# Every second weight unit of two output projections: the low part from a negated copy and an adding DMA

## The chip, the core and the metric

The kernel runs on one core of one Trainium2 chip. The metric is device time in microseconds (us) of one execution; lower is better. The engines are TensorE (PE in the profile; its weight loads are PEld), VectorE (DVE), ScalarE (ACT), GpSimd (POOL) and SyncE (SP). Transfers that SP issues and transfers that POOL issues stand in the profile as queues q1 and q0; both run on the core's 16 DMA engines.

## The reference, cut to what matters

One decoder layer, 256 tokens by 2048 channels, float32. An input projection feeds two token mixers, latent attention and a short gated convolution. Each mixer's output (256 x 2048) goes through a 2048 x 2048 branch projection, the two are merged by sigmoid gates, and an output projection follows:

```python
y_mla  = einsum('bse,ed->bsd', attn, w_o_mla)
y_conv = einsum('bse,ed->bsd', b_gate * conv * silu(z_conv), w_o_conv)
merged = sigmoid(g_mla) * y_mla + sigmoid(g_conv) * y_conv
out    = einsum('bsd,de->bse', merged, w_out)
return x + rmsnorm(out, post_norm_g)
```

The change touches the weights of the first two products, `w_o_mla` and `w_o_conv`.

## The kernel before

**Products in two parts.** TensorE multiplies in float32r here. To keep the precision, every operand is split: `hi` is the value as it comes out when written to a float32r tile, `lo` is the rest (value minus `hi`), and a product is three matmuls, hi·hi, hi·lo and lo·hi (`product`, with the matmul at L90).

**Units of weights.** All weights come in units of at most 128 x 2048 float32 (1 MB), listed in `plan` in the order in which TensorE needs them. A unit goes through three steps: SP loads it into one of three `raw` buffers (`load_raw`, L161); ScalarE writes `whi` and VectorE writes `wlo` = raw - `whi` (`split_act`, L263 and L264), each into one of three slots of its own; TensorE uses the two. `take(i)` is called where unit i is used; it calls `ahead`, which first writes down the loads and splits of the units to come. Once written, each engine works through its own queue, and a step starts when its semaphores allow. A split may start when its slot is free, that is, when the last matmul of the unit three before is done; a load may start when the split of the unit three before is done.

**The stage of the change.** `tokens(c, n, cols)` runs the branch projections: n is the branch (0 latent attention, 1 convolution), c one of four blocks of 512 output channels, and four units (kk, 0 to 3) make up one block. That is 2 x 4 x 4 = 32 units, `u_d[n][c][kk]`, each used by 24 matmuls (two token halves, four blocks of 128 inputs, three matmuls each). I count these units from 0 to 31. The input `cols` is `x_both` (n = 0) or `cv_both` (n = 1). VectorE multiplies each finished block by its gate (L1005 and L1013, L1014). In branch 1 each merged block is also transposed: `turned` turns 32 x 32 pieces on VectorE (L338), sends them to DRAM in four transfers of 64 KB per token half (`far<-sg`, L345) and brings them back in one of 256 KB (`sg<-far`, L349), all issued by POOL and kept in the written order. `features` then splits them for the output projection (`x_both<-sg`).

**Order.** The matmuls, the turning transfers and some others stand in the order of the program; the rest is ordered by the framework's scheduler. Every engine runs its own queue in order.

Of the kernel before, what the change touches and what calls it, by code (L numbers as in the profile page):

```python
# [12 lines left out]
F32R = mybir.dt.float32r  # L13
I32 = mybir.dt.int32
AF = mybir.ActivationFunctionType
ALU = mybir.AluOpType
# [68 lines left out]
def tile_layer(ctx: ExitStack, tc: tile.TileContext, xw, x, pos, pvec, post_g, wc, wz, wcv, wkr, wqk, wqr, wv, cwr, wsq, wg, out):  # L85
    nc = tc.nc
# [21 lines left out]
    plan = []  # L108

    def add(ap, width=UNIT, kind="half"):  # L110
        plan.append((ap, width, kind))
        return len(plan) - 1
# [32 lines left out]
    u_d = [[[add(wsq[n, c, k], kind="whole") for k in range(4)] for c in range(4)] for n in range(2)]  # L145
# [2 lines left out]
    out_order += [(c, k) for c in (2, 3) for k in range(4)]  # L148
    u_out = {ck: add(wsq[2, ck[0], ck[1]], kind="whole") for ck in out_order}

    raws, splits, early = {}, {}, {}
    done = {"raw": 0, "split": 0}

    def load_raw(i):
        ap, w, _ = plan[i]
        t = early.get(i)
        if t is None:
            t = wpool.tile([P, UNIT], F32, name=f"raw{i}", tag="raw", bufs=3)
        cuts = {0: (S, XW, 2 * XW), 1: (0, XW, 2 * XW), 2: (0, XW, 2 * XW)}.get(i, (0, w))
        for a, b in zip(cuts[:-1], cuts[1:]):  # L160
            nc.sync.dma_start(out=t[:, a:b], in_=ap[:, a:b])  # L161
        raws[i] = t
        if i == u_ckv[1]:
            tc.keep_in_program_order(nc.sync.dma_start(out=x_tok, in_=x))

    def slot(i, both=True):
        hi = wpool.tile([P, UNIT], F32R, name=f"whi{i}", tag="whi", bufs=3)
        return hi, wpool.tile([P, UNIT], F32R, name=f"wlo{i}", tag="wlo", bufs=3) if both else None

    def split_unit(i):  # L170
        t, (_, w, kind) = raws.pop(i), plan[i]
        if i == u_kr:
            t = t[:, :w].rearrange("p (k c) -> p k c", k=KD)
            both, parts = slot(i, False)[0], []
            for h in range(2):
                part = both[:, h * HALF : (h + 1) * HALF].rearrange("p (k j c) -> p k j c", k=KD // 2, j=2)
                split_act(part[:, :, 0], part[:, :, 1], t[:, h * KD // 2 : (h + 1) * KD // 2])
                parts.append(part.rearrange("p k j c -> p k (j c)"))
            splits[i] = parts
            return  # L180
        if i <= u_qa[-1]:

            hi, lo = slot(i)
            for j in range(2):
                k, o = 2 * i + j, j * XW
                src = x_first if k == 0 else t[:, o : o + S]
                split_scaled(x_both, src, k)
                split_act(hi[:, j * R : (j + 1) * R], lo[:, j * R : (j + 1) * R], t[:, o + S : o + XW], True)
            splits[i] = hi, lo
            return  # L190
        if u_out[3, 0] <= i < u_out[3, 3]:
            hi, lo = (op.tile([P, UNIT], F32R, name=f"w{o}{i}") for o in ("hi", "lo"))
        else:
            hi, lo = slot(i)
        if kind == "pair":
            splits[i] = split_pair(i, t, hi, lo)
            return
        n = HALF if kind == "half" else UNIT
        for h in range(0, w, n):
            e = min(h + n, w)  # L200
            split_act(hi[:, h:e], lo[:, h:e], t[:, h:e])
        splits[i] = hi, lo

    def split_pair(i, t, hi, lo):

        raw = t[:, :].rearrange("p (b c) -> p b c", b=4)
        tf = d1.tile([P, 3, 512], F32, name=f"tf{i}", tag="tf", bufs=1)
        thi, tlo = (d1.tile([P, 3, 512], F32R, name=f"t{o}{i}", tag=f"t{o}", bufs=1) for o in ("hi", "lo"))
        tt = nc.vector.tensor_tensor
        tt(tf[:, :2], raw[:, 1:3], raw[:, 0:1].to_broadcast([P, 2, 512]), op=ALU.subtract)  # L210
        tt(raw[:, 0], raw[:, 2], tf[:, 0], op=ALU.add)
        tt(tf[:, 2], raw[:, 3], raw[:, 0], op=ALU.subtract)
        split_act(hi[:, :], lo[:, :], t[:, :])
        split_act(thi[:, :, :], tlo[:, :, :], tf[:, :, :])
        w = {}
        for n, b in ((6, 0), (1, 1), (3, 2), (2, 3)):
            w[n] = [a[:, b * 512 : (b + 1) * 512] for a in (hi, lo)]
        for n, b in ((5, 0), (7, 1), (4, 2)):
            w[n] = [a[:, b] for a in (thi, tlo)]
        return w  # L220

    def ahead(i, raw=3, split=1):
        while done["raw"] < min(i + raw, len(plan)):
            load_raw(done["raw"])
            done["raw"] += 1
        while done["split"] < min(i + 1 + split, len(plan)):
            while done["raw"] <= done["split"]:
                load_raw(done["raw"])
                done["raw"] += 1
            split_unit(done["split"])  # L230
            done["split"] += 1

    def take(i):
        ahead(i)
        parts = splits.pop(i)
        if isinstance(parts, dict):
            return parts

        def piece(j, n):
            return tuple(a[:, j * n : (j + 1) * n] for a in parts)  # L240

        return piece
# [19 lines left out]
    def split_act(hi, lo, src, keep=False):  # L262
        a = nc.scalar.activation(hi, src, AF.Copy)  # L263
        b = nc.vector.tensor_tensor(lo, src, hi.bitcast(F32), op=ALU.subtract)  # L264
        if keep:

            tc.keep_in_program_order(a)
            tc.keep_in_program_order(b)
# [53 lines left out]
    n = 2 * XW // S  # L322
# [37 lines left out]
    def split_scaled(dst, src, k):  # L360
        if k == 0:
            a = nc.vector.tensor_scalar(dst[:, k, :S], src, col("pre_g", k), None, op0=ALU.mult)
        else:
            a = nc.scalar.activation(dst[:, k, :S], src, AF.Copy, scale=col("pre_g", k))
        tc.keep_in_program_order(a)
        tc.keep_in_program_order(
            nc.vector.scalar_tensor_tensor(
                dst[:, k, S:], src, col("pre_g", k), dst[:, k, :S].bitcast(F32), op0=ALU.mult, op1=ALU.subtract
            )
        )  # L370
# [150 lines left out]
    for i in range(KD // 2):  # L521
        ahead(u_qa[i], raw=3 + len(early), split=0)
        w = take(u_qa[i])
        for j in range(2):
            latent_products(ps_q, 2 * i + j, w, j)
    ps_c = [bank(f"ckv{t}") for t in range(NT)]
    for i in range(4):
        w = take(u_ckv[i])
        for k4 in range(4):
            latent_products(ps_c, 4 * i + k4, w, k4)  # L530
        if i == 0:
            next(table_parts)
        if i == 1:
            dg = input_norm()
            latent_norm("qa", ps_q)
            next(table_parts)
# [34 lines left out]
    def group_a(g):  # L571

        qn, kn = pair("qn", (P, HG, S)), temp("kn", (P, 2, HG, S), F32R, 1)
        w = take(u_grp["a", g])
        for n, src, hi, lo in (("qn", qa, qn[0], qn[1]), ("kn", ckv, kn[:, 0], kn[:, 1])):
            for j, f in enumerate(narrow([f"{n}{g}_{j}" for j in range(HG)], w, HG * (n == "kn"), src)):
                split_act(hi[:, j, :], lo[:, j, :], f[:, :])
        groups["a", g] = qn, kn
# [629 lines left out]
```

## Time and profile before

| | |
|---|---|
| median of 3 runs | 1059.69 us (1058.46 to 1060.88) |
| the profiled execution | 1061.09 us, its span 1059.3 us |
| TensorE matmul busy | 1024.0 us, 97% |
| VectorE / ScalarE / POOL busy | 742.5 / 532.5 / 180.3 us |
| granted TensorE clock, mean | 0.988 |
| the stage of the change | about 790 to 964 us of the span |

The span is what the profiler saw between the first and the last instruction; 1.8 us of the profiled time lie around it. A row `L264 DVE TENSOR_TENSOR wlo<-raw,whi ... x32 | 73.3, 2289 | 71.9 <-ACT whi L263` reads: line 264, VectorE, `wlo` made from `raw` and `whi`, 32 times; 73.3 us busy, 2289 ns each; the engine was idle for 71.9 us in front of them, mostly until ScalarE's `whi` was there.

### The profile page before, as it was taken

The page shows a single profiled execution, that of the slowest core. Times are in us where ns is not written, and L with a number is a line of the kernel's source. Part 1 is how long each engine was busy: PE and PEld are TensorE (multiplying, and loading weights), DVE is VectorE, ACT ScalarE, POOL GpSimd, SP SyncE. Part 2 cuts the span into 40 slices and gives each one's busy share as a digit, 9 for nine tenths or more (in the row PEclk, how much of TensorE's full clock was granted, in tenths as well). Part 3 has the DMA queues.
Part 4 walks back from the last instruction along what each step waited for, and adds up shares of the span by engine and source line. Part 5 has one row for each costly group of instructions (what it writes and reads, how often), then busy time and mean ns, then how long its engine had stood idle before and what let it go on. Part 6 is the DMA issues. An engine that isn't in the chain of part 4 may idle for free.

```text
span 1059.3 us, 12469 instructions
## 1 busy us (share of the span) xinstructions
PE 1024.0 (97%) x4658; PEld 851.8 (80%) x4658; DVE 742.5 (70%) x960; ACT 532.5 (50%) x675; POOL 180.3 (17%) x345
## 2 busy tenths in 40 slices
PE   9999999999999999999999839999999999999997
PEld 8887888888878888788888728888888888888885
DVE  7578769686687777777677579797976445666462
ACT  7756546455465455455555145555565333334451
POOL 7621220204202042112422210000000000232000
PEclk9999999999999999999999969999999999999999
DMA  8754766667666685656767536655555555677842
GB/s 339 299 188 176 254 221 210 219 222 277 193 230 214 214 296 182 232 208 238 267 230 231 173 113 203 216 200 214 186 211 198 194 187 186 238 250 252 321 159 79
DMA packets 41948, 231.00 MB, mean 218 GB/s; under 512 B 7520, under 2 KB 8224, under 8 KB 18976
## 3 DMA queue, kind: packets, MB, share of 16 engines
q1 hardware_dynamic: 29808, 197.54, 52.4%
q0 software_dynamic: 11648, 29.38, 9.2%
q10 hardware_dynamic: 432, 3.29, 0.7%
q8 instruction: 36, 0.59, 0.2%
q14 instruction: 24, 0.20, 0.0%
HBM read 214.48 MB, written 11.53 MB: 213 GB/s over the span
## 4 chain that ended last, share of the span: by engine, by line
PE 90%; DVE 4%; issue 2%; DMA 2%; ACT 1%; POOL 1%; DVEq 0%; POOLq 0%
PE cv L90 28%; PE sq L90 16%; PE g L90 15%; PE z L90 8%; PE out L90 8%; PE qa L90 2%; PE qn L90 2%; PE ckv L90 2%; PE kn L90 2%; DMA cw<-cwr_dram 2%; PE vv L90 2%; PE sc L90 1%; DVE wlo L264 1%; ACT whi L263 1%; PE o L90 1%
## 5 line engine op out<-in xcount | busy, mean ns | idle before, releaser
L264 DVE TENSOR_TENSOR wlo<-raw,whi 128x1024 fp32r<-128x1024 f32 (+2 forms) x290 | 423.4, 1484 | 224.7 <-ACT whi L263 223.8
L263 ACT ACTIVATE whi<-raw 128x1024 fp32r<-128x1024 f32 (+2 forms) x292 | 357.5, 1259 | 380.3 <-issue 120.5
L90 PE MATMUL cv<-whi,x_both 128*128 128x512 f32 x1024 | 323.4, 390 | 3.3 <-DVE cv_w L726 3.3
L90 PEld LDWEIGHTS cv<-whi,x_both 128*128 128x128 f32 x1024 | 192.3, 188 | 43.5 <-DVE cv_w L726 4.3
L90 PE MATMUL cv<-wlo,x_both 128*128 128x512 f32 x512 | 199.7, 390 | 0.0
L90 PE MATMUL g<-whi,x_both 128*128 128x512 f32 x368 | 119.8, 390 | 0.0
L90 PEld LDWEIGHTS cv<-wlo,x_both 128*128 128x128 f32 x512 | 96.2, 188 | 18.7
L90 PEld LDWEIGHTS g<-whi,x_both 128*128 128x128 f32 x368 | 69.4, 189 | 14.4
L90 PE MATMUL z<-whi,x_both 128*128 128x512 f32 x256 | 80.6, 390 | 0.0
L90 PE MATMUL sq<-whi,x_both 128*128 128x512 f32 x256 | 79.0, 389 | 0.0
L90 PE MATMUL sq<-whi,cv_both 128*128 128x512 f32 x256 | 78.9, 389 | 0.0
L90 PE MATMUL out<-whi,x_both 128*128 128x512 f32 x256 | 78.9, 389 | 0.0
L345 POOL DMA_DIRECT2D far<-sg x32 | 17.5, 553 | 330.4 <-DVE sg L1014 287.8
L345 POOL DMA_DIRECT2D far<-via x64 | 35.3, 559 | 225.2 <-DVE via L338 224.2
L90 PE MATMUL g<-wlo,x_both 128*128 128x512 f32 x184 | 71.8, 390 | 0.0
L90 PEld LDWEIGHTS z<-whi,x_both 128*128 128x128 f32 x256 | 48.1, 188 | 9.9
L90 PEld LDWEIGHTS sq<-whi,cv_both 128*128 128x128 f32 x256 | 48.0, 188 | 9.9
L90 PEld LDWEIGHTS out<-whi,x_both 128*128 128x128 f32 x256 | 48.0, 188 | 9.9
L90 PEld LDWEIGHTS sq<-whi,x_both 128*128 128x128 f32 x256 | 48.0, 188 | 9.9
L90 PE MATMUL z<-wlo,x_both 128*128 128x512 f32 x128 | 49.8, 389 | 0.0
L90 PE MATMUL sq<-wlo,x_both 128*128 128x512 f32 x128 | 49.8, 389 | 0.0
L90 PE MATMUL sq<-wlo,cv_both 128*128 128x512 f32 x128 | 49.8, 389 | 0.0
(243 smaller groups left out, 1325.3 us busy)
## 6 DMA issues: line engine op xcount, KB each, us to landing
raw<-wcv_dram SPq DMA_DIRECT2D x64, 1024.0 KB, 5.1
raw<-wsq_dram SPq DMA_DIRECT2D x48, 1024.0 KB, 4.8
raw<-wg_dram SPq DMA_DIRECT2D x32, 1024.0 KB, 4.8
raw<-wz_dram SPq DMA_DIRECT2D x16, 1024.0 KB, 4.8
raw<-wqk_dram SPq DMA_DIRECT2D x8, 1024.0 KB, 5.6
cw<-cwr_dram POOLq DMA_DIRECT2D x24, 256.0 KB, 7.2
raw<-wc_dram SPq DMA_DIRECT2D x4, 1024.0 KB, 9.9
raw<-wv_dram SPq DMA_DIRECT2D x4, 1024.0 KB, 5.6
```

The lines of the kernel that those rows point to most:

```text
L90: return tc.keep_in_program_order(nc.tensor.matmul(*a, **kw))
L263: a = nc.scalar.activation(hi, src, AF.Copy)
L264: b = nc.vector.tensor_tensor(lo, src, hi.bitcast(F32), op=ALU.subtract)
L345: tc.keep_in_program_order(nc.gpsimd.dma_start(out=f[i], in_=m))
```

## The change

In the stage, the units with kk = 1 and 3 (the odd ones, 16 of 32) get their low part in another way. ScalarE makes `whi` as before, and writes -1 times the raw value into `wlo`; since `wlo` is float32r, this is -`whi`. Then POOL issues a DMA that reads the raw weights once more from DRAM and adds them onto `wlo`, which gives raw - `whi`. VectorE's subtraction for these units is gone. For the units from the stage's first up to the output projection's block 3, `ahead` also writes down loads four and splits two units ahead instead of three and one.

```diff
+    by_dma = {u_d[n][c][k] for n in range(2) for c in range(4) for k in (1, 3)}
...
+        if i in by_dma:
+            nc.scalar.activation(hi[:, :], t[:, :], AF.Copy)
+            nc.scalar.activation(lo[:, :], t[:, :], AF.Copy, scale=-1.0)
+            nc.gpsimd.dma_start(out=lo[:, :], in_=plan[i][0].bitcast(F32R), accum_op=ALU.add)
+            splits[i] = hi, lo
+            return
...
     def take(i):
-        ahead(i)
+        far_ahead = u_d[0][0][0] <= i < u_out[3, 0]
+        ahead(i, raw=3 + far_ahead, split=1 + far_ahead)
```

In the rows below, the number behind a name counts the program's tiles, and what a row waits for is named by the engine or DMA lane (DMASW for POOL's transfers, DMAHW for SP's) whose semaphore it needs. ScalarE before, in the middle of the stage, one row per unit:

```order
L263 ACTIVATE whi_6863<-raw_6831 128x2048 [waits DMAHW2_49,DVE_49,PE_49]
L263 ACTIVATE whi_6897<-raw_6861 128x2048 [waits DMAHW3_49,DVE_49,PE_49]
L263 ACTIVATE whi_6927<-raw_6895 128x2048 [waits DMAHW4_49,DVE_49,PE_49]
L263 ACTIVATE whi_6957<-raw_6925 128x2048 [waits DMAHW5_49,DVE_49,PE_49]
L263 ACTIVATE whi_6987<-raw_6955 128x2048 [waits DMAHW6_49,DVE_49,PE_49]
```

ScalarE now, at the same place (L271 is the old L263):

```order
L271 ACTIVATE whi_6845<-raw_6812 128x2048 [waits DMAHW2_49,PE_49,Activation_49]
L201 ACTIVATE wlo_6876<-raw_6843 128x2048 [waits DMASW7_49,DMAHW3_49,DVE_49,PE_49]
L200 ACTIVATE whi_6875<-raw_6843 128x2048 [waits PE_49,Activation_49]
L271 ACTIVATE whi_6910<-raw_6873 128x2048 [waits DMAHW4_49,PE_49,Activation_49]
L201 ACTIVATE wlo_6941<-raw_6908 128x2048 [waits DMASW0_49,DMAHW5_49,DVE_49,PE_49]
L200 ACTIVATE whi_6940<-raw_6908 128x2048 [waits PE_49,Activation_49]
```

Every second unit now has two rows, and the negative stands ahead of the rounded copy.

TensorE before, at the first unit of branch 1, where it takes up a new `whi` and a new `wlo`:

```order
L90 MATMUL sq_1_0_7017<-whi_6987,cv_both 128x512 [waits Activation_49]
L90 MATMUL sq_1_0_7017<-wlo_6988,cv_both 128x512 [waits DVE_49]
L90 MATMUL sq_1_0_7017<-whi_6987,cv_both 128x512 x2
L90 MATMUL sq_1_0_7017<-wlo_6988,cv_both 128x512
L90 MATMUL sq_1_0_7017<-whi_6987,cv_both 128x512 x2
```

TensorE now, at the second unit of branch 1 (an odd one):

```order
L90 MATMUL sq_1_0_7032<-whi_7001,cv_both 128x512 [waits Activation_49]
L90 MATMUL sq_1_0_7032<-wlo_7002,cv_both 128x512 [waits DMASW4_49]
L90 MATMUL sq_1_0_7032<-whi_7001,cv_both 128x512 x2
L90 MATMUL sq_1_0_7032<-wlo_7002,cv_both 128x512
L90 MATMUL sq_1_0_7032<-whi_7001,cv_both 128x512 x2
```

The second matmul of an odd unit no longer waits for VectorE but for a transfer that POOL issued. The order of the matmuls is the same in both programs.

POOL before, from the first merged block of branch 1 on; until then its queue has nothing in this stage:

```order
L345 DMA far<-sg 32x4x128 [waits DVE_49,Activation_49,Pool_49]
L345 DMA far<-sg 32x4x128 x3
L345 DMA far<-sg 32x4x128 [waits DVE_49]
L345 DMA far<-sg 32x4x128
L345 DMA far<-sg 32x4x128 [waits DMASW2_49]
L345 DMA far<-sg 32x4x128 [waits DMASW3_49]
L349 DMA sg<-far 128x512 [waits DMASW6_49,DMASW7_49,DMASW5_49,DMASW4_49]
L349 DMA sg<-far 128x512 [waits DMASW2_49,DMASW3_49,DMASW1_49,DMASW0_49]
```

POOL now, at the same place (L353 and L357 are the old L345 and L349, L202 is the adding DMA):

```order
L202 DMA wlo_7067<-wsq_dram 128x2048 [waits DMASW2_49,Activation_49]
L202 DMA wlo_7128<-wsq_dram 128x2048 [waits DMASW3_49,Activation_49]
L353 DMA far<-sg 32x4x128 [waits DVE_49,Pool_49]
L353 DMA far<-sg 32x4x128 x3
L353 DMA far<-sg 32x4x128 [waits DVE_49]
L353 DMA far<-sg 32x4x128 [waits DMASW4_49]
L353 DMA far<-sg 32x4x128 [waits DMASW5_49]
L353 DMA far<-sg 32x4x128 [waits DMASW6_49]
L357 DMA sg<-far 128x512 [waits DMASW2_49,DMASW7_49,DMASW1_49,DMASW0_49]
L202 DMA wlo_7209<-wsq_dram 128x2048 [waits Activation_49]
L357 DMA sg<-far 128x512 [waits DMASW5_49,DMASW6_49,DMASW4_49,DMASW3_49]
L202 DMA wlo_7270<-wsq_dram 128x2048 [waits Activation_49]
```

Eleven adding DMAs stand ahead of the first turning transfer, and the other five between the turning transfers; three of these (`wlo_7209` is the first) come behind one `sg<-far` and ahead of the next.

## The prediction, as put on record before the changed kernel ran

> **What bounds the kernel now.** I read the page's busy shares first, then the chain of work that ended last, then the stage of the change by groups, by engine and by queue.
>
> ```profile
> span 1059.3 us, 12469 instructions
> PE 1024.0 (97%) x4658; PEld 851.8 (80%) x4658; DVE 742.5 (70%) x960; ACT 532.5 (50%) x675; POOL 180.3 (17%) x345
> 628.14 162.30 PE g L90 x707
> 790.44 174.08 PE sq L90 x768
> 964.52 87.05 PE out L90 x384
> L264 DVE TENSOR_TENSOR wlo<-raw,whi 128x2048 fp32r<-128x2048 f32 x32 | 73.3, 2289 | 71.9 <-ACT whi L263 71.8
> L263 ACT ACTIVATE whi<-raw 128x2048 fp32r<-128x2048 f32 x32 | 61.3, 1917 | 100.1 <-PE sq L90 96.9 <-issue 3.0 <-ACT cv_both L263 0.2
> ```
>
> The first two rows are the page's: TensorE is busy 97% of the span. The next three are the end of the chain (start, length): from 628 us on it is TensorE alone, without a gap, and the branch projections (`sq`) are 174.08 us of it, 768 matmuls at 0.2267 us, 5.44 us per unit. The last two rows are groups of this stage alone: VectorE makes 32 low parts at 2.29 us and ScalarE 32 high parts at 1.92 us; ScalarE waits for TensorE to free slots. So VectorE, which the change relieves, is not what this stage waits for. A gain would need a TensorE wait that goes away, and there is none; what can change the time is a low part that comes late.
>
> How much room a low part has, from the timeline (start, length):
>
> ```profile
> 790.28 0.39 PE L90 MATMUL sq<-whi,x_both 128*128 128x512 f32 x1
> 790.50 0.39 PE L90 MATMUL sq<-wlo,x_both 128*128 128x512 f32 x1
> 834.00 1.92 ACT L263 ACTIVATE whi<-raw 128x2048 fp32r<-128x2048 f32 x1 [3.52 <-PE sq L90]
> 835.95 2.29 DVE L264 TENSOR_TENSOR wlo<-raw,whi 128x2048 fp32r<-128x2048 f32 x1 [1.26 <-ACT whi L263]
> ```
>
> Unit 0's first low matmul is at 790.50. Unit 7's last matmul ends at 790.28 + 191 x 0.2267 + 0.39 = 833.97, and ScalarE starts the split of unit 10, which takes unit 7's slot, at 834.00. Unit 10's first low matmul comes at 790.50 + 10 x 5.44 = 844.9. So a split has 10.9 us. Before, it used 4.24 of them (done at 838.24), with 6.7 us to spare.
>
> **The change part by part.**
>
> Removed: 16 subtractions of 2.29 us, 36.6 us of VectorE, all beside TensorE. Worth nothing on the path.
>
> Added on ScalarE: 16 negatives. The same engine, shape and number of operands as the row of 1.92 us, so 30.7 us, in a stage where ScalarE is idle for 100 us in front of its high parts alone. The high part of an odd unit now ends at 834.00 + 2 x 1.92 = 837.84 instead of 835.92; it is needed at 844.7. Nothing on the path.
>
> Loads: the raw buffer of an odd unit is freed by ScalarE at 837.84 instead of by VectorE at 838.24, 0.4 us earlier. SP's waits in the stage are only for these buffers, and a load lands in 4.8 us, some 7 us before unit 13's split at 850.3: covered. The longer look-ahead adds nothing of its own, since split and load already start when slots free them.
>
> Added on POOL: 16 adding DMAs of 1 MB. No row shows an adding DMA; these are the nearest, with the median time from issue to landing:
>
> ```profile
> raw<-wsq_dram SPq DMA_DIRECT2D x32, 1024.0 KB, 4.8
> far<-sg POOLq DMA_DIRECT2D x24, 64.0 KB, 3.0
> sg<-far POOLq DMA_DIRECT2D x6, 256.0 KB, 4.3
> ...
> raw<-wqr_dram SPq DMA_DIRECT2D x8, 256.0 KB, 2.6
> ...
> q1 hardware_dynamic: 4608, 33.56, 54.8%
> q0 software_dynamic: 1248, 3.15, 6.0%
> ...
> 990.00:1000.00 10.00, 10.00 (x46) 8.29 (x45) 4.07 (x3) 3.92 (x3) 0.00 (x0) 1.00 1.01 419
> ```
>
> All but the wqr and the last row are of this stage. SP's 256 KB land in 2.6 us and its 1 MB in 4.8: 768 KB more cost 2.2. POOL's 256 KB take 4.3, so a plain 1 MB from POOL is 4.3 + 2.2 = 6.5 us. Adding must read what lies in `wlo` as well, a second 1 MB through the same engines. In the last row (window, four engines' busy time, clock, DMA share, GB/s) the engines were full and moved 419 GB/s, so 1 MB at its cheapest is 2.5 us; by the queue's row SP's load holds the engines for 54.8% of 5.44 = 2.98 us. The second read costs 2.5 to 2.98; I take 2.5, since it follows work already queued: 9.0 us. Then it meets loads: the add leaves at 834.00 + 1.92 = 835.9, one load was issued at about 832.8 and is nearly in, the next is freed at 837.84, in the middle of the add. They share 16 engines, so between nothing and a whole load, 2.98 us, is added; I take half, 1.5. Together D = 10.5 us from issue to landing; the ends are 6.5 (no cost of the second read, no meeting) and 6.5 + 2.98 + 2.98 = 12.5.
>
> The room for D is 10.9 - 1.92 = 9.0, less 0.03 for each of two handovers (the row pair above: high part done at 835.92, VectorE starts at 835.95), so 8.9 us. At D = 10.5 the first low part is x = 1.6 us late. The next one is helped by that: odd unit j gets its slot when unit j-3 ends, ahead of unit j-2, whose stall widens j's room. So two stalls in a row add up to x, 0.8 us per odd unit on average: 16 x 0.8 = 12.8 us. A check by throughput, per two units of 10.88 us: two loads 2 x 2.98, the add 2.98 + 2.5, turning 6.0% of 10.88 = 0.65, together 12.1, 1.2 us too much, 19 us in 16 pairs; at 2.5 us per MB throughout, 10.65, nothing too much. The 12.8 lies between.
>
> The Trainium skill (Collectives: The Full Stack, "The bandwidth ceiling: the fold count and why AG ≠ RS ≠ AR") says that a reducing transfer runs at half a copy's rate, since the add needs two source reads on one ring and the adding itself is free. By it the second read would cost the whole 2.98, D = 11.0 and the sum 16.8 us; no run here shows it.
>
> Sum: the profiled execution, 1061.09 us (span 1059.3 and 1.8 around it), becomes 1073.9. It stands 1.4 us above the median of 1059.69 and 0.2 above the highest of the three runs; the terms are differences, so against the median: 1059.69 + 12.8 = 1072.5 us. The bound D = 12.5 gives x = 3.6 and 28.8 us: 1088.5. A measurement of this kernel can tell about 0.2%, 2.1 us, from no change.
>
> POOL's queue holds nothing but this in branch 0. In branch 1, `wlo_7209` and two more adds stand behind an `sg<-far` that waits for its turning transfers:
>
> ```profile
> 904.44 2.17 POOL L345 DMA_DIRECT2D far<-sg  x4 [1.01 <-DVE sg L338]
> 906.60 0.56 POOL L349 DMA_DIRECT2D sg<-far  x1
> 910.20 0.56 POOL L349 DMA_DIRECT2D sg<-far  x1 [3.04 <-DMA far<-sg]
> ```
>
> That add's negative is ready at 790.28 + 21 x 5.44 + 0.4 + 1.92 = 906.8, while POOL is done with the first `sg<-far` at 907.16. So three adds go out some 0.4 us late, 0.6 us in all by the halving above; I leave that out of the sum, and name the case where it grows below.
>
> **The rivals.**
>
> Hidden after all: D stays under 8.9 because the second read runs beside the first inside the DMA engines. For it: 6.5 lies 2.4 below the limit, and 9.0 is at it. Against: the stage's engines are already 63% busy, and adds raise that. Then nothing waits: 1059.7. It decides at D = 8.9.
>
> The add is much slower than a copy, say a quarter of its rate: D = 6.5 + 3 x 2.98 + 2.98 = 18.4, x = 9.5, 76 us: 1136. Nothing in the profile speaks for or against. Then the clock joins in:
>
> ```profile
> 600.00:604.00 4.00, 1.65 (x9) 1.46 (x10) 3.65 (x6) 0.38 (x1) 0.00 (x0) 1.00 0.02 4
> 612.00:616.00 4.00, 0.00 (x0) 0.00 (x0) 3.45 (x6) 1.03 (x3) 0.55 (x1) 0.50 0.47 131
> 628.00:632.00 4.00, 3.86 (x9) 3.07 (x10) 2.70 (x4) 1.84 (x1) 0.00 (x0) 0.52 0.75 295
> ```
>
> With 1.65 of 4 us busy the granted clock (third number from the end) stayed 1.00; after several idle us it was 0.50, and 0.52 for the first 4 us of work. Stalls of 1 us leave it alone; stalls near 5 us may cost 2 us more each, 32 us: 1168. The Trainium skill (TensorE: Matmul & The Clock Gate, "What's actually happening") puts the point at one idle window of about 3.4 us; by that, and these rows agree, my likeliest case keeps its clock.
>
> POOL's order: the five adds of the late blocks wait behind turning transfers that are slower among the adds. A `far<-sg` or `sg<-far` late by 1 to 2 us, in five places, gives 3 to 8 us by itself: 1065.
>
> Faster: it would need a TensorE wait that VectorE ends, and no row of the stage has one.
>
> **How the numbers follow.** Late adds, D 9.3 to 12.5: 0.45, with 1063 to 1088.5 as its own range. Hidden: 0.33. Slow add: 0.12. POOL's order alone: 0.07. Faster for a reason I don't see: 0.03. Predicted is the likeliest, 1072.5. The range starts at 1058 (hidden, with the runs' spread). It ends at 1100, where the add runs at a third of a copy's rate (D = 6.5 + 2 x 2.98 + 1.5 = 14.0, x = 5.1, 41 us); beyond lies most of the slow case. Slower by over 0.2%: 0.45 + 0.12 + 0.07, less some late adds of under 2.1 us in all: 0.61. Within: 0.36. Faster: 0.03.
>
> **What would show it.** In the changed profile: VectorE's group at 128x2048 in this stage has 16 rows less; ScalarE has 16 `wlo<-raw` rows of 1.92 us; the issues show 16 `wlo<-wsq_dram` of 1024 KB on POOL's queue, their landing time is D. The waits show TensorE `sq` waiting for that DMA, 16 times at most, about 0.8 us each, and the chain of this stage no longer is TensorE alone. The stage lasts 174 + 13 us at a clock of 1.00. I am wrong if that landing time is under 8.9 us and TensorE waits nowhere, if the waits are there but fall on branch 1 alone (POOL's order), or if they exceed 3.6 us each.

## The result, and the profile after

The changed kernel takes 1085.24 us (median of 3 runs, 1083.62 to 1085.25) against 1059.69 before: 1.0237 times as long, 95% interval 1.0217 to 1.0257. Forecast were 1072.5 us, slower, with a range of 1058 to 1100. The profiled execution took 1083.62 us.

From the page of the changed kernel: the span, the busy times, the engines' shares of the chain that ended last, and the row of the adding DMAs (count, KB each, median us from issue to landing).

```profile
span 1081.8 us, 12516 instructions
PE 1032.8 (95%) x4658; PEld 854.0 (79%) x4658; DVE 708.5 (65%) x944; ACT 561.1 (52%) x691; POOL 195.2 (18%) x361
PE 74%; issue 11%; DMA 7%; DVE 5%; POOL 2%; ACT 1%; DVEq 0%; POOLq 0%
wlo<-wsq_dram POOLq DMA_DIRECT2D x16, 1024.0 KB, 10.2
```

VectorE lost 34.0 us of work, ScalarE gained 28.6, and transfers now stand on the chain. The stage's end in the chain (start, length):

```profile
908.28 6.65 DMA far<-sg
916.11 11.77 DMA wlo<-wsq_dram
927.92 7.16 PE sq L90 x23
...
951.89 5.54 PE sq L90 x23
...
967.25 12.31 DMA wlo<-wsq_dram
979.60 7.41 PE sq L90 x23
987.01 87.05 PE out L90 x384
```

The output stage lasts 87.05 us as before; all the loss lies ahead of it. From the first `sq` matmul at 789.44 to 987.01 are 197.6 us, where the chain before had 174.08: 23.5 us. The waits of TensorE's weight loads in the stage (total us, times, longest):

```profile
PEld sq L90 <- DMA wlo<-wsq_dram: 21.5, 13, 5.4
```

By branch, the first row up to 884 us, the second from there on:

```profile
PEld sq L90 <- DMA wlo<-wsq_dram: 8.5, 7, 2.1
PEld sq L90 <- DMA wlo<-wsq_dram: 13.0, 6, 5.4
```

Behind the two longest waits the clock is lower as well. The chain's 23 matmuls take 7.16 and 7.41 us there, and 5.54 behind the short wait at 951.89: some 3.5 us more in all. Waits and clock together make 25.0, so the waits overstate by about 1.5 us what they cost. The windows of branch 0 and branch 1, and of 6 us behind the first and around the end of the second of these waits (busy time of PE, PEld, DVE, ACT and POOL, then granted clock, DMA share, GB/s):

```profile
789.50:884.10 94.60, 88.89 (x385) 71.46 (x384) 30.23 (x26) 50.94 (x36) 6.88 (x8) 1.00 0.94 269
884.10:986.90 102.80, 92.35 (x386) 74.10 (x385) 38.63 (x36) 46.63 (x29) 22.79 (x37) 0.95 0.93 281
930.00:936.00 6.00, 6.00 (x22) 4.80 (x22) 3.47 (x6) 1.48 (x2) 1.01 (x2) 0.79 1.01 277
978.00:984.00 6.00, 4.40 (x11) 3.52 (x12) 2.00 (x3) 0.63 (x1) 0.00 (x0) 0.53 0.83 337
```

Branch 0 took 7.6 us more than its 87, branch 1 15.7 more. The DMA share, 0.55 in branch 0 before, is 0.94. Everything that shares the engines lands later (785 to 985 us; before, these were 4.8, 3.0 and 4.3 us):

```profile
raw<-wsq_dram SPq DMA_DIRECT2D x33, 1024.0 KB, 7.8
far<-sg POOLq DMA_DIRECT2D x24, 64.0 KB, 5.4
sg<-far POOLq DMA_DIRECT2D x6, 256.0 KB, 9.0
```

Two theories were left. **L**, the forecast's: each add by itself takes longer than the room that its slot leaves. **F**: over a pair of units the DMA engines have more work than the pair's 10.88 us hold, so something is late whatever the room. Beside them stood POOL's order, for the two long stalls.

### The profile page after: what moved, and what is told of

It reads as the page before. It is cut to its first block, busy times and chain, and to the rows that moved or that the text cites. A ratio compares the mean times of both kernels' runs of the same rounds, so it can differ in the third digit from the quotient of the medians.

```text
span 1081.8 us, 12516 instructions
## 1 busy us (share of the span) xinstructions
PE 1032.8 (95%) x4658; PEld 854.0 (79%) x4658; DVE 708.5 (65%) x944; ACT 561.1 (52%) x691; POOL 195.2 (18%) x361
## 4 chain that ended last, share of the span: by engine, by line
PE 74%; issue 11%; DMA 7%; DVE 5%; POOL 2%; ACT 1%; DVEq 0%; POOLq 0%
PE cv L90 27%; PE g L90 15%; PE z L90 8%; PE out L90 8%; DMA wlo<-wsq_dram 4%; PE sq L90 3%; PE qn L90 2%; PE qa L90 2%; PE ckv L90 2%; PE kn L90 2%; DMA cw<-cwr_dram 2%; PE vv L90 2%; DVE wlo L272 1%; PE sc L90 1%; DMA far<-sg 1%
## 5 line engine op out<-in xcount | busy, mean ns | idle before, releaser
L272 DVE TENSOR_TENSOR wlo<-raw,whi 128x1024 fp32r<-128x1024 f32 (+2 forms) x274 | 386.9, 1437 | 226.3 <-ACT whi L271 225.4
L271 ACT ACTIVATE whi<-raw 128x1024 fp32r<-128x1024 f32 (+2 forms) x276 | 326.8, 1221 | 319.3 <-issue 128.6
L90 PE MATMUL cv<-whi,x_both 128*128 128x512 f32 x1024 | 323.4, 390 | 2.9 <-DVE cv_w L734 2.9
L90 PEld LDWEIGHTS cv<-whi,x_both 128*128 128x128 f32 x1024 | 192.3, 188 | 43.0 <-DVE cv_w L734 4.0
L90 PE MATMUL cv<-wlo,x_both 128*128 128x512 f32 x512 | 199.7, 390 | 0.0
L90 PE MATMUL g<-whi,x_both 128*128 128x512 f32 x368 | 121.0, 394 | 0.0
L90 PEld LDWEIGHTS cv<-wlo,x_both 128*128 128x128 f32 x512 | 96.2, 188 | 18.8
L90 PEld LDWEIGHTS g<-whi,x_both 128*128 128x128 f32 x368 | 70.2, 191 | 14.8
L90 PE MATMUL sq<-whi,cv_both 128*128 128x512 f32 x256 | 81.7, 400 | 0.0
L90 PE MATMUL z<-whi,x_both 128*128 128x512 f32 x256 | 80.6, 390 | 0.0
L90 PE MATMUL sq<-whi,x_both 128*128 128x512 f32 x256 | 79.1, 389 | 0.0
L90 PE MATMUL out<-whi,x_both 128*128 128x512 f32 x256 | 78.9, 389 | 0.0
L353 POOL DMA_DIRECT2D far<-via x64 | 35.3, 558 | 221.5 <-DVE via L346 220.6
L90 PE MATMUL g<-wlo,x_both 128*128 128x512 f32 x184 | 72.4, 393 | 0.0
L202 POOL DMA_DIRECT2D wlo<-wsq_dram x16 | 14.0, 878 | 300.8 <-ACT wlo L201 298.5
L90 PE MATMUL sq<-wlo,cv_both 128*128 128x512 f32 x128 | 52.0, 406 | 10.4 <-DMA wlo<-wsq_dram 10.4
L90 PEld LDWEIGHTS sq<-whi,cv_both 128*128 128x128 f32 x256 | 49.7, 194 | 10.6
L90 PE MATMUL sq<-wlo,x_both 128*128 128x512 f32 x128 | 50.6, 395 | 5.7 <-DMA wlo<-wsq_dram 5.7
L90 PEld LDWEIGHTS out<-whi,x_both 128*128 128x128 f32 x256 | 48.0, 188 | 9.9
L90 PEld LDWEIGHTS z<-whi,x_both 128*128 128x128 f32 x256 | 48.1, 188 | 9.9
L90 PEld LDWEIGHTS sq<-whi,x_both 128*128 128x128 f32 x256 | 48.1, 188 | 9.9
L201 ACT ACTIVATE wlo<-raw 128x2048 fp32r<-128x2048 f32 x16 | 30.6, 1914 | 48.0 <-PE sq L90 45.0
## 6 DMA issues: line engine op xcount, KB each, us to landing
wlo<-wsq_dram POOLq DMA_DIRECT2D x16, 1024.0 KB, 10.2
```

The costliest lines, as they stand in the source:

```text
L90: return tc.keep_in_program_order(nc.tensor.matmul(*a, **kw))
L201: nc.scalar.activation(lo[:, :], t[:, :], AF.Copy, scale=-1.0)
L202: nc.gpsimd.dma_start(out=lo[:, :], in_=plan[i][0].bitcast(F32R), accum_op=ALU.add)
L353: tc.keep_in_program_order(nc.gpsimd.dma_start(out=f[i], in_=m))
```

## The experiments

Differences in us are against the kernel before, run on the same chip beside each.

### Copying instead of adding

```diff
-            nc.gpsimd.dma_start(out=lo[:, :], in_=plan[i][0].bitcast(F32R), accum_op=ALU.add)
+            nc.gpsimd.dma_start(out=lo[:, :], in_=plan[i][0].bitcast(F32R))
```

> The DMA of the odd units copies the raw weights over wlo instead of adding them (the subtraction is left out: wlo holds the raw weights). Traffic from DRAM, queue, size and waits are the same as in the changed kernel. Theory A (adding costs a second read in the DMA engines): landing falls from 10.2 us to about 7 to 8 us, below the room of 8.9 us, TensorE's waits for wlo go away but for units 23 and 31, where POOL's order holds the DMA back: 1060 to 1067 us. Rival B (the cost is the crowd of transfers, not the adding): landing stays at 9.5 us or more and the time above 1075 us.

This kernel leaves out the subtraction. Measured: 1061.95 us, +2.3, ratio 1.0020 (1.0011 to 1.0030). From its page, and the only wait of TensorE's matmuls in the stage:

```profile
wlo<-wsq_dram POOLq DMA_DIRECT2D x16, 1024.0 KB, 5.2
PE sq L90 <- DMA wlo<-wsq_dram: 2.2, 1, 2.2
```

Same queue, same place of the returns (`sg<-far`) among POOL's transfers, same bytes from DRAM, and nearly the whole loss is gone: it is the adding. ScalarE's 16 negatives, the look-ahead and POOL's order are in this kernel too, so with plain copies they come, together with one wait of 2.2 us, to no more than 2.3 us. Theory A's landing of 7 to 8 us was itself too high.

### One branch at a time

```diff
-    by_dma = {u_d[n][c][k] for n in range(2) for c in range(4) for k in (1, 3)}
+    by_dma = {u_d[n][c][k] for n in (0,) for c in range(4) for k in (1, 3)}
```

> Only the eight odd units of branch 0 get the adding DMA, where POOL's queue holds nothing else; branch 1 as before the change. Theory (lateness alone there, 8.5 us of TensorE waits in the changed kernel's branch 0): 1059.7 + 8 = 1067 to 1069 us. If the two branches' delays push each other, it would be nearer to 1065 or 1072.

Measured: 1065.60 us, +6.0, ratio 1.0056 (1.0037 to 1.0076). That is 1.4 us under the range that was expected; the single runs lie between 1063 and 1068. Branch 0 costs by itself what it cost in the changed kernel, 7.6 us, within the interval (4 to 8 us).

With `n in (1,)`:

> Only the eight odd units of branch 1 get the adding DMA. Theory (lateness, about 1.06 us per add as in branch 0, plus two stalls of 4 to 5 us at units 23 and 31 behind POOL's sg<-far, plus 2 us of lower clock after them): 1059.7 + 15 to 16 = 1075 us. Rival (branch 1 was only slower since branch 0 had left it behind): 1059.7 + 8 = 1068 us.

Measured: 1073.37 us, +13.8, ratio 1.0130 (1.0113 to 1.0147). The rival falls: branch 1 is the dearer one by itself, and its two long waits are there too (5.4 and 3.9 us at the weight loads). The sum of both, 19.8, stays 4 to 6 us below the changed kernel's 24.0 and 25.6 (it was run twice).

### The adds ahead of the turning transfers

```diff
+            if kk == 1:
+                for come, dst in late:
+                    come(dst)
...
-        for t, (_, come) in enumerate(steps):
-            come(m[t])
+        late = [(come, m[t]) for t, (_, come) in enumerate(steps)]
```

> All 16 adds as in the changed kernel, but the two returns (sg<-far) of blocks 0 to 2 of branch 1 are written after unit kk = 1 of the next block, so on POOL's queue the adds of units 23, 27 and 31 stand ahead of them. Theory (POOL's order makes the two stalls of 3.9 and 4.9 us): both shrink to about 1 us, the clock stays at 1.00: 1085 - 2.9 - 3.9 - 2 = 1076 us. Rival (these stalls come from the traffic of the turning transfers, not from the order): 1083 to 1086 us.

Measured: 1077.69 us, +18.1, ratio 1.0178 (1.0161 to 1.0195). POOL's timeline around the add of unit 23, in the changed kernel and then in this one (start, length, what the wait before it was for):

```profile
915.56 0.56 POOL L357 DMA_DIRECT2D sg<-far  x1 [1.75 <-DMA far<-sg]
916.11 0.94 POOL L202 DMA_DIRECT2D wlo<-wsq_dram  x1
```

```profile
914.77 0.92 POOL L202 DMA_DIRECT2D wlo<-wsq_dram  x1 [0.66 <-ACT wlo L201]
915.94 0.57 POOL L357 DMA_DIRECT2D sg<-far  x1 [0.25 <-issue]
```

In the changed kernel this unit's negative was done at 911.76 + 1.91 = 913.67, and the add left 2.4 us later, behind the `sg<-far`. Taken out, the longest stall of the stage is 2.6 us (5.4 before), and 6 to 7.5 us come back against the two runs of the changed kernel. So POOL's order has a real part. But 18 us stay, and the total wait is still `PEld sq L90 <- DMA wlo<-wsq_dram`, 16.3 us in 13 waits.

### Half as many adds

With `for k in (1,)`:

> Only kk = 1 gets the adding DMA, 8 of 32 units, so four units of 21.8 us carry four loads and one add instead of two. By the engines' time (4 x 2.98 for the loads, 2 x 2.98 for one add, some 1.3 for turning: 19 us) they are no longer full. Theory F (the adds are late because the DMA engines are full over a pair of units): TensorE waits nowhere, 1060 us. Rival L (each add by itself takes longer than the room, 9.5 us as in branch 0 alone, against some 8.4): 8 stalls of about 1 us, no neighbour to share them, 1066 to 1068 us.

Measured: 1063.48 us, +4.0, ratio 1.0032 (1.0020 to 1.0044).

```profile
PEld sq L90 <- DMA wlo<-wsq_dram: 3.9, 8, 0.7
DMA to landing us min/median/max: 8.8/9.1/9.3
```

Here both theories get something. With the engines no longer full, all eight adds are still late, by 0.5 us each: that is L, and all of it (a landing of 9.1 us, so the room was 8.6 rather than 8.9). L's 1066 to 1068 was too much, F's 1060 too little. Twice as many adds cost not twice but six times as much. Part of that factor is POOL's order, since the adds that it holds back in the changed kernel (units 23, 27 and 31) all have kk = 3 and are not in this one; against the 18.1 us with the order mended it is 4.5 times.

### More room for the adds

From unit 11 on (in block 2 of branch 0), odd units write into two slots of their own:

```diff
+        if extra and i in by_dma:
+            return hi, extra[0].tile([P, UNIT], F32R, name=f"wlod{i}", tag="wlod", bufs=2)
```

> From block 2 of branch 0 on, the odd units' low parts lie in two slots of their own beside the three of the even units, so the negative and the add can start about one unit (5.4 us) earlier; traffic is the same. Theory L (the add is longer than its room): no TensorE wait from unit 11 on, what is left are the first five adds' stalls, about 4 us: 1063 to 1066 us. Rival F (the DMA engines are full whatever the room; 94% busy in the changed kernel's stage of 197.6 us, so at 100% the stage would last 186 us instead of 174): 1070 to 1078 us.

Measured: 1082.31 us, +22.9, ratio 1.0211 (1.0196 to 1.0226). The waits of TensorE's matmuls in the stage:

```profile
PE sq L90 <- DVE wlo L276: 7.4, 5, 1.8
PE sq L90 <- DMA wlod<-wsq_dram: 5.9, 2, 4.5
PE sq L90 <- DMA wlo<-wsq_dram: 1.5, 2, 1.0
PE sq L90 <- ACT whi L275: 0.9, 1, 0.9
...
raw<-wsq_dram SPq DMA_DIRECT2D x12, 1024.0 KB, 9.7
...
931.76 1.92 ACT L205 ACTIVATE wlod<-raw 128x2048 fp32r<-128x2048 f32 x1 [8.78 <-DMA raw<-wsq_dram]
```

The row of the raw loads is of 884 to 960 us. L is refuted as the main cause: with some 5 us more room the time hardly falls. From unit 11 on all adds but two come in time, and now the even units are late, because the raw loads take 9.7 us to land, where they took 7.9 in these 76 us of the changed kernel and 4.8 before. The wait moved from one transfer to the other. It was worse than F's 1070 to 1078. The longest wait, 4.5 us at unit 25, is again one for a load: the last row is this unit's negative, which stood 8.8 us for its raw weights, and the add left right behind it, at 933.97. POOL's order in branch 1 was another again, and what that did stays open.

### Half of the loads left out

```diff
+        if u_d[0][0][2] <= i <= u_d[1][3][2] and i not in by_dma:
+            raws[i] = kept[0]
+            return
```

> From unit 2 of the stage to its end the even units are not loaded; they are split from the raw buffer of the odd unit before them (the load of their own weights is left out). The adds stay as they are, with half of the loads out of their way. Theory L with the forecast's terms (6.5 for a copy, 2.5 for the second read, 1.5 for the load in the way): landing falls by 1.5 us, to about 8.7, stalls of 0 to 0.4 us, and only POOL's order is left: 1062 to 1067 us. Theory F: engines at 60 to 70%, landing near 7 us, 1060 to 1064 us. Rival (adding itself is the slow part, whatever else runs): landing stays at 9.5 us or more, 1075 us or more.

Measured: 1062.18 us, +2.7, ratio 1.0035 (1.0017 to 1.0052); single runs went up to 1067. The add lands in 7.9/8.0/10.5 us (least, median, most) instead of 10.2, under the room, with 2 waits of TensorE's matmuls left (1.7 us together). The returns stand on POOL's queue where the changed kernel has them. The adding DMA is not too slow by itself; it is so beside two loads. The queues' rows from 790 to 878 us (branch 0 alone; packets, MB, share of the 16 engines), of this kernel, then of the one with plain copies:

```profile
q0 software_dynamic: 1177, 8.59, 53.7%
q1 hardware_dynamic: 1152, 8.39, 26.5%
```

```profile
q1 hardware_dynamic: 2343, 17.10, 52.4%
q0 software_dynamic: 1152, 8.39, 28.4%
```

In 88 us, an add (1024 KB, 1.049 MB) holds the engines for 0.537 x 88 / 8.59 x 1.049 = 5.77 us, a plain copy from POOL for 3.12, a load for 2.8 to 2.9. The changed kernel's own rows of these 88 us give somewhat less, 5.49 for an add and 2.72 for a load:

```profile
q0 software_dynamic: 1104, 8.00, 47.6%
q1 hardware_dynamic: 2163, 15.76, 46.4%
```

### Half of each add

```diff
+            nc.scalar.activation(lo[:, :HALF], t[:, :HALF], AF.Copy, scale=-1.0)
+            nc.gpsimd.dma_start(out=lo[:, :HALF], in_=plan[i][0][:, :HALF].bitcast(F32R), accum_op=ALU.add)
+            nc.vector.tensor_tensor(lo[:, HALF:], t[:, HALF:], hi[:, HALF:].bitcast(F32), op=ALU.subtract)
```

> All 16 odd units, but only the first 1024 columns get the negative and the adding DMA; VectorE subtracts the other 1024. POOL issues as many DMAs at the same places, each half as long. Theory F: 2 x 2.98 + 2.5 + 0.85 = 9.3 us of engine time in 10.88, landing of about 5.5 us, TensorE waits only where POOL's order holds an add for 2 us or more: 1060 to 1063 us. Rival (an add costs by its number, not by its bytes, or POOL's order costs by itself): 1068 us or more.

Measured: 1061.38 us, +2.8, ratio 1.0024 (1.0015 to 1.0034). The add lands in 5.2/5.5/8.1 us, as expected, and the profiled execution has no wait of TensorE in the stage. So the number of adds costs little by itself: the bytes do. On POOL's order this run says nothing, against what was expected of it. The scheduler has put the adds of units 23, 27 and 31 ahead of the returns here; around unit 23:

```profile
905.52 0.96 POOL L202 DMA_DIRECT2D wlo<-wsq_dram  x1
906.12 0.94 POOL L358 DMA_DIRECT2D sg<-far  x1
```

That the order costs little while the transfers land early is shown by the kernel with plain copies and by the one with half of the loads, which have it. Where the 2 to 3 us come from that the runs show and the profiled one (span 1058.3) does not, stays open.

### Two copies and no adding

```diff
+            nc.gpsimd.dma_start(out=lo[:, :], in_=plan[i][0].bitcast(F32R))
+            if extra:
+                spare = extra[0].tile([P, UNIT], F32R, name=f"spare{i}", tag="spare", bufs=2)
+                nc.scalar.activation(spare[:, :8], t[:, :8], AF.Copy)
+                nc.gpsimd.dma_start(out=spare[:, :], in_=plan[i][0].bitcast(F32R))
```

> As the kernel with plain copies (the subtraction is left out), and from unit 11 on each odd unit issues a second plain copy of the same 1 MB from POOL into a spare SBUF buffer that nobody reads: 11 of 16 pairs carry two loads and two copies and no add. Theory F (an adding DMA hurts because it holds the engines for about as long as two copies): 2 x 2.7 + 2 x 2.9 + 0.85 = 12.1 us of engine time in 10.88, TensorE waits in those pairs, 1061.95 + 11 x 1.2 = 1075 us, 1070 to 1080. Rival (adding is slow in a way of its own): TensorE waits no more than with one copy, 1060 to 1065 us.

This kernel leaves out the subtraction too, and the second copies run from unit 11 on. Measured: 1071.65 us, +12.2, ratio 1.0100 (1.0074 to 1.0126). From 845 to 980 us, where the second copies are:

```profile
q0 software_dynamic: 4321, 24.54, 49.3%
q1 hardware_dynamic: 3264, 23.73, 45.8%
...
raw<-wsq_dram SPq DMA_DIRECT2D x23, 1024.0 KB, 8.8
wlo<-wsq_dram POOLq DMA_DIRECT2D x10, 1024.0 KB, 10.3
```

Without any addition the picture of the changed kernel is back: engines 95% busy, loads at 8.8 us, `wlo` at 10.3, and 12.5 us of TensorE waits. The spare copy of the odd unit before mostly goes out 4 to 6 us ahead of the one that is waited for, on the same queue, so part of this can be order. How much is not shown; but no adding is needed for the picture.

### The look-ahead, and the changed kernel again

```diff
-        ahead(i, raw=3 + far_ahead, split=1 + far_ahead)
+        ahead(i)
```

> The longer look-ahead is undone (loads three and splits one unit ahead, as before the change), the adds stay. Theory (a step starts when its slot allows, so the look-ahead did nothing): 1085 us, within 3 us. Rival (it moved POOL's adds ahead of turning transfers, or loads into the adds' way): another 5 us up or down.

> The changed kernel once more, beside the next two. If the 6.5 us that the kernel without the longer look-ahead stood below it are real: 1083 to 1086 us. If its first three runs stood high by chance: 1078 to 1083 us.

> The adds of units 23, 27 and 31 ahead of the sg<-far on POOL's queue, and the longer look-ahead undone as well. Theory F (the DMA engines carry some 12.1 us of work in 10.88 us, so 16 pairs need about 19 us more whatever the order): no better than with the first of the two edits alone, 1077 to 1079 us. Rival (the two edits take away different waits): 7.5 + 6.5 us below the changed kernel, 1071 us.

Measured: 1078.68 us without the look-ahead (+19.2, ratio 1.0184, 1.0155 to 1.0214); 1082.62 for the changed kernel again (+24.0, 1.0223, 1.0204 to 1.0242); 1080.31 for the third (+21.7, 1.0215, 1.0197 to 1.0233). In the third the edit on `come` did nothing: with the short look-ahead the add of unit 23 is written down after the returns again, and POOL's queue has the order of the changed kernel. So it is a second sample without the look-ahead, and settles nothing on combining the two edits. The four runs of the changed kernel lie between 1078.8 and 1084.7 here, so part of the 6.5 us that were asked about is its spread from run to run. Undoing the look-ahead is worth between nothing and about 6 us; the intervals overlap, and it stays open.

## Why the prediction was right, and where it was off

**Right.** That TensorE would become the one that waits, for the low part of odd units, and that little else of the change matters: with plain copies in place of the adds, VectorE's relief, ScalarE's added work, the look-ahead and the plain traffic come to 2.3 us together. The landing time, 10.2 us against D = 10.5. The clock stayed at 1.00 behind the waits of under 2 us. And the size of the late adds in branch 0, as the table below shows.

**Right by terms that made up for each other.** D was 6.5 for a copy, 2.5 for the second read and 1.5 for a load in the way. The copy landed in 5.2 us with loads beside it, where the first and third terms gave 8.0. The add lands 2.8 us later than that with half the loads gone (8.0) and 5.0 later with all of them (10.2). So the term for the second read was about right in size, though no run shows that it is a read, and the loads in the way cost an add at least 2.2 us where 1.5 stood. D is no fixed property of an add: the busier the engines, the later it lands. The page that the prediction named (the Trainium skill, Collectives: The Full Stack, "The bandwidth ceiling: the fold count and why AG ≠ RS ≠ AR") has the reduce step of ring collectives at half a copy's rate. This adding DMA is no ring collective, but its engine times agree, 5.5 to 5.8 us for an add against 2.7 to 3.1 for a copy or a load.

**The step that failed** is branch 1. The sum gives both branches the same, 8 x 0.8 = 6.4 us, and leaves POOL's order out at 0.6 us. The waits of TensorE's weight loads, in us:

| | branch 0 | branch 1 |
|---|---|---|
| forecast | 6.4 | 6.4 |
| the changed kernel | 8.5 | 13.0 |
| the same, second time | 7.0 | 12.2 |
| the adds ahead of the turning transfers | 6.4 | 9.8 |
| one branch at a time | 6.6 | 12.4 |

Branch 0 comes out at the forecast or up to 2.1 us above it; most of what is missing lies in branch 1, for two reasons.

The first is POOL's order. The mechanism was named, at the right place; its size rests on the turning transfers, which the prediction took at their old speed in the sum (the rival had them 1 to 2 us late). Behind full engines they land in 5.4 and 9.0 us, POOL stands at `sg<-far`, and the adds of units 23 and 31 go out 2.4 and 2.7 us behind their negatives, with no room left. They end the two long waits:

```profile
927.92 0.19 PEld L90 LDWEIGHTS sq<-wlo,cv_both 128*128 128x128 f32 x1 [4.33 <-DMA wlo<-wsq_dram]
979.60 0.29 PEld L90 LDWEIGHTS sq<-wlo,cv_both 128*128 128x128 f32 x1 [5.36 <-DMA wlo<-wsq_dram]
```

The third add behind a `sg<-far`, unit 27's, left only 0.3 us late. The two long waits are 9.7 of the 21.5 us, and both then lower the clock. The 14 other odd units have 11.8 us, 0.84 each, where the forecast had 0.8. That they meet it so closely is in part luck: the rule behind it, two stalls in a row that add up to 1.6, does not hold unit by unit (units 11, 13 and 15 waited 2.1, 1.7 and 1.3 us).

The second reason shows once the order is mended: that returns 6 to 7.5 us and no more, while the waits for the other six adds of branch 1 grow from 3.3 to 6.7 us. Branch 1 then still waits 9.8 us. Its engines have the turning transfers to carry as well, 12.0% of 87 us, or 1.3 per pair of units, as before the change:

```profile
q0 software_dynamic: 1248, 3.15, 12.0%
```

The prediction's check by throughput (12.1 us of work in 10.88, 19 us) spread them evenly over both branches, at 6.0%. That these 1.3 us make the difference between the branches was not tested by itself.

**What a sum of engine time gives.** With the prices from the kernel with half of the loads, a pair in branch 0 needs 2 x 2.9 + 5.77 = 11.6 us, 0.7 too much, 5.5 us over the branch's 8 pairs; in branch 1 it needs 12.9, 2.0 too much, 16 us. Together that is 21.5 us. With the changed kernel's own prices (5.49 and 2.72) a pair in branch 0 needs 10.9 us and about fits, one in branch 1 needs 12.2, and together 11 us are too much. Measured are 18.1 us with POOL's order mended. So the sum says which branch is the dearer one and brackets the loss, but it does not give its size.

The rival "hidden after all" put the engines at 63% busy before the change; the windows of the stage have 0.55 and 0.67, 0.61 on average. Nothing hangs on it.

**Of the signs of being wrong**, one came half true: two of the thirteen waits exceeded 3.6 us, the others did not. These two are POOL's order, which another of the signs had named.

## What to carry to other kernels

The adding DMA held the DMA engines about twice as long as a copy of its size here (5.5 to 5.8 us against 2.7 to 3.1). Before moving an engine's work onto one, add up all transfers of a period, with that price, against the period, and do so for each stage with its own transfers. If the sum is at the period or over it, expect that some transfer is late. More buffers did not help here, they only moved the wait from the adds to the loads (22.9 us of loss against 24.0 and 25.6); another order of the queue did, by 6 to 7.5 us. Where a queue issues in order, look at what stands ahead of a transfer that has no room, and how late that will be once the engines are full.

## What the runs showed that was not expected

The point at which a stall lowers the clock is not sharp. Behind waits of the weight loads of 2.56 us (the kernel with the adds ahead of the turning transfers) and 2.60 us (the one with plain copies), the granted clock fell to about a half; behind one of 2.67 us (the changed kernel, second time) it did not. The windows right behind these three waits, in this order:

```profile
808.20:810.20 2.00, 1.99 (x5) 1.61 (x6) 0.60 (x1) 1.68 (x1) 0.51 (x1) 0.50 1.00 234
```

```profile
937.60:939.60 2.00, 1.99 (x6) 1.59 (x7) 0.58 (x1) 2.00 (x2) 0.16 (x1) 0.63 1.00 371
```

```profile
976.70:978.70 2.00, 2.00 (x9) 1.66 (x10) 2.00 (x2) 0.64 (x1) 0.00 (x0) 1.00 0.99 420
```

The Trainium skill (TensorE: Matmul & The Clock Gate, "What's actually happening") has the clock drop after one idle window of about 3.4 us, and the window running free of the kernel. That a wait of one length falls on both sides agrees with a window that runs free; that 2.6 us were enough in two cases is less than its figure, and here the measurement decides. The loss is small: in both cases the clock was back at 1.00 within 4 us.
